# A three-block transformer kernel: in its first stage two held loads hang on other squares, one tile's weights load later, and all input sums run on Vector

## The chip, the cores and the metric

The kernel runs on one core of one Trainium2 chip. That core has a matrix engine (PE, with its weight loads as PEld), three engines for elementwise work (VectorE or DVE, ScalarE or ACT, GpSimd or POOL), and SP, which here issues all loads. Each engine works through its instructions in order. The metric is the device time of one execution in microseconds, as the median of several runs.

## The reference, cut to what matters

Two blocks run one after the other on 512 tokens of width 1024, in f32. Only the beginning of the first is touched by the change:

```python
mod = silu(c) @ ada_w + ada_b                # nine vectors of 1024
sh1, sc1, gt1, sh2, sc2, gt2, sh3, sc3, gt3 = split(mod, 9)
u = modulate(rmsnorm(h, norm1_w), sh1, sc1)  # h * (1 + scale) + shift
h = h + 0.5 * gt1 * swiglu(u, ffn1_w_in, ffn1_w_out)   # hidden width 2816
```

Behind it come the attention and retention mixers, a second feed-forward, and the second block with two more feed-forwards.

## The kernel before

**Numbers.** PE multiplies f32 values that are split into a high and a low half. A product is three matmuls: high by high, high by low, low by high. The halves of the input are `uh` and `ul`, those of a weight chunk `whi` and `wlo`. ACT makes each high half (`hi`, L230), DVE or POOL subtracts to get the low half (`lo`, L238 or L240).

**Start (method `start`).** All its instructions keep their written order on each engine (`pin`). SP loads the input as eight tiles `h[k]`. ACT squares each one, DVE adds the squares up, and `rstd` and `bcast` make the factor `R` from the sum. The vectors `sc1` and `sh1` come from eight "pairs" `apair` of 1 MB each (function `load`); DVE multiplies both halves of pair k by the row `cr`, which lies in PSUM, and sums (function `dots`, here: product k). With them DVE scales tile k (`unorm0`, tile `un`), ACT makes `uh` and a shifted copy, and POOL makes `ul`. Three pair buffers and three buffers for raw weights rotate, so a later load waits on SP until its buffer is free, and all that stands behind it on SP waits too. The loads of pairs 0 and 1 are held: `act` lets ACT write one element of the buffer first, so the load cannot be issued before ACT has come to that place. Four weight chunks, for hidden tiles 0 and 1 ("the first pair" of tiles; each tile has a chunk for the gate and one for the value), are loaded between the pairs (`wraw`) and split (`wsplit`). Behind product 5 ACT copies `cr` to SBUF as `crow`; product 6 waits for this copy.

**Feed-forward (method `ffn`).** Tiles 0 and 1 are multiplied in the order `FIRST`. Then `W=5` makes tiles 2, 3 and 4 run "whole": two chunks, 48 matmuls of 512 columns each. From tile 5 on the tiles run as units of seven half-size products, mixed with units of the output product. The units need sums and differences of four quarters of the input: `b` = `uh` + `ul` per quarter (L657), four differences (`bparts`, L497), and their halves; the fourth set rewrites a quarter of `uh` and `ul`, behind tile 4. In `CFG[0]` the letters of `UT` choose the engine of the four sums, `UE` of the four differences and `ULO` of the four low halves: `p` is POOL, `d` is DVE. Each unit also sums and subtracts its weights on POOL (`in_open`, tiles `ws`, `rb`, `raw`).

**Ada rows.** The other vectors of `mod` are computed row by row beside this: SP loads a row `araw` of 0.5 MB into one of two buffers and DVE multiplies it by `crow` and sums (L302). The list `ADA` says how many rows are issued at each place: its first entry ahead of tiles 0 and 1, then behind them, behind each of tiles 2 to 4, and then one per unit.

**Order.** Outside the pinned parts a scheduler with a model of the time decides the order on each engine. `issue_after(x)` keeps what is written in its block behind x on x's own engine only. `self.mark` holds two such instructions: the load of `identb`, last on SP in `start`, and the last `un` on DVE:

```python
x = self.unorm0(KT - 1, R)
self.mark = [nc.sync.dma_start(self.identb, a["constb"][:, 0:P]), x]
```

Of the kernel before, what the change touches and what calls it, by code (L numbers as in the profile page):

```python
# [17 lines left out]
S = 512  # L18
# [3 lines left out]

FIRST = [(k, j) for k in (0, 1) for j in (0, 1)] + [(k, j) for j in (2, 3) for k in (0, 1)] + [(k, j) for k in range(2, 8) for j in range(4)]
SPLIT = ((0, 4), (4, 4), (8, 4), (12, 4), (16, 6))
HP, ARB, ADA = 200, 2, (0, 3, 3, 2) + (1,) * 17

CFG = (dict(SENG='pppp', UT='pdpp', UE='ddpp', ULO='dddp', CF=(1, 1, 2, 4), W=5, LEAD=2),
       dict(SENG='pppp', UT='ddpd', UE='dddd', ULO='dddd', CF=(2, 2, 2, 4), W=3, LEAD=2),
       dict(SENG='pdpp', UT='pdpd', UE='ddpp', ULO='pdpp', CF=(1, 1, 2, 4), W=3, LEAD=2),
       dict(SENG='pppp', UT='pdpp', UE='ddpd', ULO='dddd', CF=(1, 1, 2, 4), W=3, LEAD=2))  # L30
# [127 lines left out]
class Builder:  # L158
# [232 lines left out]
    def norm(self, blk, st, a, sh=None, eng="dve"):  # L391
        c0, n = blk
        R = self.bcast(self.rstd(self.msq([st], n)[0], n), n)
        for k in range(KT):
            e = eng[k] if len(eng) == KT else "d"
            self.unorm(k, c0, n, a, sh, R, self.t(self.npool, [P, 264], F32, "unorm", bufs=3)[:, :n], {"p": "pool", "d": "dve"}[e])

    def unorm(self, k, c0, n, a, sh, R, u, eng="dve"):
        nc = self.nc
        uh, ul = self.uh[:, k, c0:c0 + n], self.ul[:, k, c0:c0 + n]  # L400
        nc.vector.scalar_tensor_tensor(u, self.h[:, k, c0:c0 + n], a[:, k:k + 1], R, op0=ALU.mult, op1=ALU.mult)
        if sh is None:
            self.hi(uh, u)
            self.lo(ul, u, uh, eng)
        else:
            nc.scalar.activation(uh, u, AF.Identity, bias=sh[:, k:k + 1])
            nc.vector.scalar_tensor_tensor(ul, u, sh[:, k:k + 1], uh.bitcast(F32), op0=ALU.add, op1=ALU.subtract)
# [72 lines left out]
    def out_open(self, wo, m, f0, nk):  # L480

        R = self.t(self.wp, [P, 1024], F32, "raw", bufs=3)
        for i in range(2):
            with self.tc.high_priority(HPD):
                self.nc.sync.dma_start(R[:, 512 * i:512 * i + nk * P], wo[m + i][:, f0 * P:(f0 + nk) * P])
        wh, wl = (self.t(self.wp, [P, 1024], F32R, x) for x in ("whi", "wlo"))
# [49 lines left out]
    def ffn(self, idx, wa, wb, wo, coef, first, blocks, last, stat, done, ada=(), late=False, half=None, opened=None, start=None, wl="dve"):  # L536
# [9 lines left out]
        (c0, n), (c1, _) = half  # L546
        self.cfg = CFG[idx]
        self.cf, whole_to, lead = (self.cfg[x] for x in ("CF", "W", "LEAD"))
        with ExitStack() as ctx:
# [10 lines left out]
            def close(f):  # L560

                g[f] = gtile()
                src = gx[f][:, :, :n]
                h, l = (x.rearrange("p (b n) -> p b n", b=2) for x in g[f])
                self.hi(h, src)
                self.lo(l, src, h)
# [53 lines left out]
            def whole(fs, ws, order=None):  # L620
                for bc, bn in first:
                    pts = self.group(ws, self.uh, self.ul, bc, bn, order=order)
                    for j, f in enumerate(fs):
                        if f not in gx:
                            gxt(f)
                        for b, c in ((0, c0), (1, c1)):
                            if bc <= c < bc + bn:
                                s = gx[f][:, b, :n]
                                nc.scalar.activation(s, pts[2 * j][:, c - bc:c - bc + n], AF.Silu)
                                nc.vector.tensor_tensor(s, pts[2 * j + 1][:, c - bc:c - bc + n], s, op=ALU.mult)  # L630

            if ada:
                ap = self.pool("ada", ctx=ctx)
            cst = ctx.enter_context(ExitStack())
            ws = start(cst) if start else [self.wchunk(w(f), 1024, wl) for f in range(2) for w in (wa, wb)]
            f1 = len(ws) // 2
            if ada:
# [33 lines left out]
                close(f)  # L671
            for f in range(f1, whole_to):
                with ExitStack() as c:
                    if start:
                        c.enter_context(self.tc.issue_after(self.mark[1].ins))
                    ws = [self.wchunk(w(f), 1024) for w in (wa, wb)]
                whole([f], ws)
                close(f)
                self.ada_after(ada.pop(0) if ada else 0)
# [392 lines left out]
    def ret(self, xp, mp, st, oh, ol, raw, other):  # L1072
# [15 lines left out]
        for i in range(N + AH + 3):  # L1088
# [31 lines left out]
            if 0 <= k < N:  # L1120
                t, r, j = units[k]
                n = S - P * j
                start = j == 0
                if start:
                    po = self.ps("po")
                for y in s_.pop(k):
                    mm(po[:, P * j:], st["rv"][:, j, 2 * t + r, :], y[:, :n], start=start, stop=True, skip_group_check=True)
                    start = False
                if j == 3:
                    if r == 0:  # L1130
                        ot = self.t(mp, [P, S], F32, "ot", bufs=1)
                    self.fold(mp, ot, r, po)
                    if r == 1:
                        late.append((i + 2, self.ret_norm(mp, t, st, ot, oh, ol)))
# [646 lines left out]
    def start(self, wsrc):  # L1781

        nc, a = self.nc, self.a
        nc.pin(True)
        c = self.t(self.ap, [1, D], F32, "c0")
        nc.sync.dma_start(self.vecs, a["vecs"])
        nc.sync.dma_start(c, a["crow"])
        nc.sync.dma_start(self.cst, a["consts"])
        for k in range(KT):
            nc.sync.dma_start(self.h[:, k, NM:L], a["xT"][k])  # L1790
        nc.scalar.activation(c, c, AF.Silu)
        self.sqrtset()

        cr = self.psum.tile([P, D], F32, tag="pl", name=self.nm("pl"), bufs=1)
        for i in range(2):
            nc.tensor.matmul(cr[:, S * i:S * i + S], self.con("ones")[0:1, :], c[:, S * i:S * i + S], start=True, stop=True)
        pt = self.ps("aux")
        raws = {}

        def load(k, gate=None):  # L1800

            raws[k] = self.t(self.ap, [P, 2, D], F32, "apair", bufs=3)
            if gate is not None:
                gate(raws[k][0:1, 0, 0:1])
            return nc.sync.dma_start(raws[k].rearrange("p a b -> p (a b)"), a["ada_c"][k])

        def act(o):
            nc.scalar.activation(o, self.eps[0:1, :], AF.Copy)

        def dots(k):  # L1810

            sc, sh = (self.mod[v][:, k:k + 1] for v in (1, 0))
            for j, m in ((0, sc), (1, sh)):
                nc.vector.scalar_tensor_tensor(raws[k][:, j], raws[k][:, j], 1.0, cr, op0=ALU.mult, op1=ALU.mult, accum_out=m)
            nc.scalar.activation(sc, sc, AF.Identity, scale=self.mod_w(1, k, 1), bias=s1[:, k:k + 1])
            nc.scalar.activation(sh, sh, AF.Identity, bias=self.vec("ada_b", k, 1))

        for k in range(KT):
            if k == 6:
                load(0, act)  # L1820
            sq = self.t(self.ap, [P, S], F32, "sqa0") if k == 0 else self.t(self.ap, [P, S], F32, "sq0", bufs=3)
            nc.scalar.activation(sq, self.h[:, k, NM:L], AF.Square)
            if k:
                nc.vector.tensor_tensor(acc, acc, sq, op=ALU.add)
            else:
                acc = sq
        for i in range(4):
            nc.tensor.matmul(pt[:, i:i + 1], acc[:, i * P:i * P + P], self.con("ones")[:, 0:1], start=True, stop=True)

        s1 = self.t(self.ap, [P, KT], F32, "s1")  # L1830
        nc.vector.scalar_tensor_tensor(s1, self.vec("ada_b", 8, 8), 1.0, self.vec("norm1_w"), op0=ALU.add, op1=ALU.mult)
        R = self.bcast(self.rstd(pt[:, 0:4], S), S)
        ws = [self.wraw(wsrc[0])]
        load(1, act)
        ws += [self.wraw(wsrc[1]), self.wraw(wsrc[2])]
        load(2)
        dots(0)
        ws[0] = self.wsplit(ws[0], self.wx)
        self.unorm0(0, R, lambda: ws.__setitem__(0, ws[0]("pool")))
        ws.append(self.wraw(wsrc[3]))  # L1840
        for k in range(1, KT):
            dots(k)
            if k < 6:
                load(k + 2)
            if k < 4:
                ws[k] = self.wsplit(ws[k], self.wx if k == 1 else None)
            if k > 1:
                self.unorm0(k - 1, R)
            if k < 4:
                ws[k] = ws[k]("pool")  # L1850
            if k == 5:
                nc.scalar.activation(self.crow, cr, AF.Copy)
        x = self.unorm0(KT - 1, R)
        self.mark = [nc.sync.dma_start(self.identb, a["constb"][:, 0:P]), x]
        return ws
# [79 lines left out]
```

## Time and profile before

| | us |
|---|---|
| median of 3 runs | 2374.49 |
| lowest and highest | 2372.78, 2375.73 |
| the profiled execution | 2369.6 |
| its span | 2367.8 |

The profile shows one execution. Its chain of work that ended last runs through PE for 72% of the span and through DVE for 12%. PE is busy for 2247.1 us, DVE for 1620.2 us, ACT for 1131.6 us and POOL for 927.9 us. The stage in question is the first 110 us. In the views an instruction is named by its line, the tile that it writes and the tiles that it reads; `x2` counts instructions that are merged in a row. The brackets give the engine's idle time before the instruction and what ended it. PEclk is the clock granted to PE, as a share of 2.4 GHz.

### The profile page before, as it was taken

How to read it: one execution, taken by the hardware profiler on the slowest of the kernel's cores; microseconds unless marked ns; L12 is line 12 of the kernel's file. 1: busy time of each engine (PE TensorE's matmuls, PEld its weight loads, DVE VectorE, ACT ScalarE, POOL GpSimd, SP SyncE). 2: the span in 40 equal slices, each digit the busy share in tenths (PEclk: the TensorE clock that was granted, in tenths of full speed). 3: DMA queues.
4: the chain of work that ended last, by engine and by line, in shares of the span. 5: the costliest groups of instructions: out<-in, count | busy, mean ns of one | idle time of the engine just before them, and what ended most of it. 6: DMA issues, size and time to landing. Idle time of an engine off the chain costs nothing.

```text
span 2367.8 us, 39220 instructions
## 1 busy us (share of the span) xinstructions
PE 2247.1 (95%) x15328; PEld 2073.3 (88%) x15328; DVE 1620.2 (68%) x2432; ACT 1131.6 (48%) x2005; POOL 927.9 (39%) x787
## 2 busy tenths in 40 slices
PE   6899999999999989999996999999999999999998
PEld 4799999888877879899996899999998888999998
DVE  6877776356665857766657776666578886866664
ACT  5344445355545234444445444444466664544443
POOL 4434442133332212544438643333334434544442
PEclk9999999999999999999997899999999999999999
DMA  8533336211143862333322133332322223232332
GB/s 298 169 125 120 124 103 188 75 37 36 56 141 95 261 214 72 107 107 99 107 71 81 35 100 107 99 99 70 124 84 63 71 68 107 92 97 98 101 94 83
DMA packets 95227, 253.29 MB, mean 107 GB/s; under 512 B 16641, under 2 KB 23425, under 8 KB 93762
## 3 DMA queue, kind: packets, MB, share of 16 engines
q1 hardware_dynamic: 95042, 250.79, 33.7%
q8 instruction: 120, 1.97, 0.3%
q14 instruction: 65, 0.53, 0.1%
HBM read 238.03 MB, written 6.29 MB: 103 GB/s over the span
## 4 chain that ended last, share of the span: by engine, by line
PE 72%; DVE 12%; DMA 5%; issue 5%; ACT 3%; POOL 3%; SPq 0%; DVEq 0%; ACTq 0%; POOLq 0%
PE mA L138 22%; PE mB L138 18%; PE mm L138 7%; PE pl L138 5%; PE at L138 3%; DVE wlo L238 3%; PE mA L270 2%; PE mA L271 2%; PE mA L272 2%; PE mB L272 2%; PE mB L271 2%; PE mB L270 2%; DMA araw<-in_ada_r_dram 2%; PE po L138 1%; PE tp L138 1%
## 5 line engine op out<-in xcount | busy, mean ns | idle before, releaser
L230 ACT ACTIVATE whi<-raw 128x1024 fp32r<-128x1024 f32 (+2 forms) x285 | 292.6, 1031 | 317.9 <-PE mB L138 119.7
L238 DVE TENSOR_TENSOR wlo<-raw,whi 128x1024 fp32r<-128x1024 f32 (+2 forms) x257 | 336.4, 1312 | 96.0 <-ACT whi L230 94.7
L138 PE MATMUL mA<-uh,whi 128*128 128x256 f32 (+2 forms) x1004 | 292.2, 291 | 18.9 <-ACT unorm L572 10.0
L138 PE MATMUL mA<-uh,wlo 128*128 128x256 f32 (+2 forms) x1004 | 290.1, 289 | 5.0 <-DVE wlo L238 3.4
L138 PE MATMUL mA<-ul,whi 128*128 128x256 f32 (+2 forms) x1004 | 289.7, 289 | 2.9 <-POOL ul L138 2.9
L463 POOL TENSOR_TENSOR ws<-raw,rb 128x512 f32<-128x512 f32 x74 | 107.3, 1450 | 289.4 <-DMA rb<-in_ffn_w_in_dram 97.4
L138 PEld LDWEIGHTS mA<-uh,whi 128*128 128x128 f32 x1004 | 191.3, 191 | 27.8 <-ACT unorm L572 14.5
L138 PEld LDWEIGHTS mA<-uh,wlo 128*128 128x128 f32 x1004 | 191.1, 190 | 8.1 <-DVE wlo L238 4.4
L138 PEld LDWEIGHTS mA<-ul,whi 128*128 128x128 f32 x1004 | 191.2, 190 | 6.7 <-POOL ul L138 4.4
L475 POOL TENSOR_TENSOR raw<-raw,ws 128x512 f32<-128x512 f32 x74 | 101.4, 1370 | 215.8 <-DVE wlo L238 126.4
L593 POOL TENSOR_TENSOR gx<-gx,unorm 128x256 f32<-128x256 f32 (+1 forms) x74 | 68.0, 918 | 224.8 <-ACT gx L592 224.8
L138 PE MATMUL mB<-uh,wlo 128*128 128x256 f32 (+2 forms) x524 | 153.1, 292 | 2.2 <-POOL wlo L138 2.2
L138 PE MATMUL mB<-uh,whi 128*128 128x256 f32 (+2 forms) x524 | 152.7, 291 | 0.0
L138 PE MATMUL mB<-ul,whi 128*128 128x256 f32 (+2 forms) x524 | 152.7, 291 | 0.0
L238 DVE TENSOR_TENSOR wlo<-rb,whi 128x1024 fp32r<-128x1024 f32 x74 | 113.5, 1534 | 45.5 <-ACT whi L230 45.5
L238 DVE TENSOR_TENSOR wlo<-ws,whi 128x1024 fp32r<-128x1024 f32 x74 | 126.2, 1706 | 17.1 <-ACT whi L230 16.9
L230 ACT ACTIVATE whi<-rb 128x1024 fp32r<-128x1024 f32 x74 | 77.9, 1052 | 105.2 <-PE mB L138 58.4
L138 PE MATMUL mm<-uh,whi 128*128 128x264 f32 (+2 forms) x368 | 125.0, 340 | 1.2 <-DVE sks L1504 1.2
L465 POOL TENSOR_TENSOR rb<-rb 128x512 f32<-128x512 f32 x74 | 125.0, 1689 | 1.1
L352 POOL TENSOR_TENSOR sqacc<-sqacc,sqt 128x256 f32<-128x256 f32 (+2 forms) x84 | 79.3, 965 | 113.6 <-ACT sqt L347 113.3
L238 DVE TENSOR_TENSOR gl<-gx,gh 128x512 fp32r<-128x512 f32 (+1 forms) x88 | 68.9, 786 | 75.9 <-ACT gh L230 75.9
L138 PE MATMUL mm<-uh,wlo 128*128 128x264 f32 (+2 forms) x368 | 120.8, 328 | 0.0
(537 smaller groups left out, 7717.8 us busy)
## 6 DMA issues: line engine op xcount, KB each, us to landing
araw<-in_ada_r_dram SPq DMA_DIRECT2D x56, 512.0 KB, 4.5
raw<-in_ffn_w_in_dram SPq DMA_DIRECT2D x52, 512.0 KB, 3.8
raw<-in_ffn_w_gate_dram SPq DMA_DIRECT2D x44, 512.0 KB, 3.8
rb<-in_ffn_w_up_dram SPq DMA_DIRECT2D x38, 512.0 KB, 3.6
rb<-in_ffn_w_in_dram SPq DMA_DIRECT2D x36, 512.0 KB, 3.6
raw<-in_wA_dram SPq DMA_DIRECT2D x36, 512.0 KB, 3.7
raw<-in_ffn_w_out_dram SPq DMA_DIRECT2D x64, 256.0 KB, 3.4
raw<-in_ffn_w_down_dram SPq DMA_DIRECT2D x64, 256.0 KB, 3.0
```

The lines of the kernel that those rows point to most:

```text
L138: ins = f(*args, **kw)
L230: nc.scalar.activation(out, src, AF.Copy)
L238: self.nc.vector.tensor_tensor(out, src, hi.bitcast(F32), op=ALU.subtract)
L270: mm(ps, wh, xh, start=first, stop=False)
L271: mm(ps, wh, xl, start=False, stop=False)
L272: mm(ps, wl, xh, start=False, stop=last)
L352: nc.gpsimd.tensor_tensor(st["acc"], st["acc"], s, op=ALU.add)
L463: E[3].tensor_tensor(s3, A[:, 0:512], b1, op=ALU.subtract)
L465: E[1].tensor_tensor(b1, b1, b2, op=ALU.add)
L475: E[4].tensor_tensor(a2, a2, s2, op=ALU.subtract)
L593: nc.gpsimd.tensor_tensor(y, y, u["z"], op=ALU.mult)
```

## The change

Five edits, all in the first feed-forward. In `CFG[0]` all letters of `UT`, `UE` and `ULO` become `d`: three sums, two differences and one low half go from POOL to DVE. `ADA` gets a second zero in front, so that no rows are issued behind the first pair and three, three, two behind tiles 2, 3 and 4. The chunks of tile 2 to 4 are kept behind both marks instead of the second alone, so on SP behind `identb`. In `start` pair 0 is held by the third square instead of the sixth, and pair 1 by the eighth square instead of the square root in `rstd`, whose lines move behind it.

```diff
-HP, ARB, ADA = 200, 2, (0, 3, 3, 2) + (1,) * 17
-
-CFG = (dict(SENG='pppp', UT='pdpp', UE='ddpp', ULO='dddp', CF=(1, 1, 2, 4), W=5, LEAD=2),
+HP, ARB, ADA = 200, 2, (0, 0, 3, 3, 2) + (1,) * 17
+
+CFG = (dict(SENG='pppp', UT='dddd', UE='dddd', ULO='dddd', CF=(1, 1, 2, 4), W=5, LEAD=2),
...
             for f in range(f1, whole_to):
                 with ExitStack() as c:
-                    if start:
-                        c.enter_context(self.tc.issue_after(self.mark[1].ins))
+                    for m in self.mark if start else ():
+                        c.enter_context(self.tc.issue_after(m.ins))
                     ws = [self.wchunk(w(f), 1024) for w in (wa, wb)]
...
         for k in range(KT):
-            if k == 6:
+            if k == 3:
                 load(0, act)
...
-        R = self.bcast(self.rstd(pt[:, 0:4], S), S)
         ws = [self.wraw(wsrc[0])]
         load(1, act)
+        R = self.bcast(self.rstd(pt[:, 0:4], S), S)
         ws += [self.wraw(wsrc[1]), self.wraw(wsrc[2])]
```

What this does to the order shows on two engines. On SP, behind the loads of pairs 3 and 4 (`apair`), with `raw` the chunks of tiles 2, 3 and 4 in turn and `araw` the ada rows:

```order
 L138 DMA apair_210<-in_ada_c_dram 128x2048
-L245 DMA raw_460<-in_ffn_w_in_dram 128x1024
 L138 DMA apair_226<-in_ada_c_dram 128x2048
 L138 DMA apair_242<-in_ada_c_dram 128x2048
-L245 DMA raw_466<-in_ffn_w_in_dram 128x1024
 L138 DMA apair_254<-in_ada_c_dram 128x2048
 L138 DMA identb_84<-in_constb_dram 128x128
```

The two chunks of tile 2 leave their places between the pairs; in the new order they are the first rows behind `identb`, ahead of the first two ada rows.

On DVE, behind the last `un`, before the change:

```order
L302 SCALAR_TENSOR_TENSOR araw_402,mod_15_90<-araw_402,crow_74 128x1024
L302 SCALAR_TENSOR_TENSOR araw_405,mod_15_90<-araw_405,crow_74 128x1024
L238 TENSOR_TENSOR wlo_463<-raw_460,whi_462 128x1024
L238 TENSOR_TENSOR wlo_469<-raw_466,whi_468 128x1024
L657 TENSOR_TENSOR b_95_435<-uh_82,ul_83 128x1024
L302 SCALAR_TENSOR_TENSOR araw_408,mod_15_90<-araw_408,crow_74 128x1024
L302 SCALAR_TENSOR_TENSOR araw_531,mod_15_90<-araw_531,crow_74 128x1024
L497 TENSOR_TENSOR b_94_433<-b_95_435,b_94_433 128x1024
L138 TENSOR_TENSOR gx_391<-mB_292,gx_391 128x256 x2
L238 TENSOR_TENSOR wlo_543<-raw_540,whi_542 128x1024
```

and with it, where `wlo_454` and `wlo_460` belong to tile 2 and `wlo_534` to tile 3:

```order
L238 TENSOR_TENSOR wlo_454<-raw_451,whi_453 128x1024
L238 TENSOR_TENSOR wlo_460<-raw_457,whi_459 128x1024
L302 SCALAR_TENSOR_TENSOR araw_522,mod_15_90<-araw_522,crow_74 128x1024
L302 SCALAR_TENSOR_TENSOR araw_525,mod_15_90<-araw_525,crow_74 128x1024
L657 TENSOR_TENSOR b_91_424<-uh_82,ul_83 128x1024
L657 TENSOR_TENSOR b_92_426<-uh_82,ul_83 128x1024
L657 TENSOR_TENSOR b_93_428<-uh_82,ul_83 128x1024
L657 TENSOR_TENSOR b_94_430<-uh_82,ul_83 128x1024
L138 TENSOR_TENSOR gx_391<-mB_292,gx_391 128x256 x2
L302 SCALAR_TENSOR_TENSOR araw_528,mod_15_90<-araw_528,crow_74 128x1024
L497 TENSOR_TENSOR b_91_424<-b_92_426,b_91_424 128x1024
L238 TENSOR_TENSOR wlo_534<-raw_531,whi_533 128x1024
```

DVE now does all four sums in a row, one ada row fewer ahead of tile 3's first low half, and eight instead of nine ada rows ahead of tile 4's.

## Rows read from the trace of the kernel before

**Rows 1.** Profile page, part 1: busy us of each engine (share) and instructions.
```profile
PE 2247.1 (95%) x15328; PEld 2073.3 (88%) x15328; DVE 1620.2 (68%) x2432; ACT 1131.6 (48%) x2005; POOL 927.9 (39%) x787
```
**Rows 2.** Timeline of PE, tiles 2 to 4: start, us, instruction [idle before, releaser].
```profile
57.35 0.40 PE L270 MATMUL mA<-uh,whi 128*128 128x512 f32 x1
...
68.72 0.40 PE L271 MATMUL mA<-ul,whi 128*128 128x512 f32 x1
...
70.12 0.50 PE L272 MATMUL mA<-uh,wlo 128*128 128x512 f32 x1 [1.00 <-DVE wlo L238]
...
71.92 0.72 PE L272 MATMUL mB<-uh,wlo 128*128 128x512 f32 x1 [0.84 <-DVE wlo L238]
...
88.19 0.50 PE L272 MATMUL mA<-uh,wlo 128*128 128x512 f32 x1 [4.02 <-DVE wlo L238]
...
89.99 0.80 PE L272 MATMUL mB<-uh,wlo 128*128 128x512 f32 x1 [0.84 <-DVE wlo L238]
...
90.58 0.63 PE L270 MATMUL mA<-uh,whi 128*128 128x512 f32 x1
...
95.70 0.50 PE L270 MATMUL mA<-uh,whi 128*128 128x512 f32 x1
```
**Rows 3.** Chain of waits, where the units begin: start, us, what.
```profile
102.91 1.41 PE mA L138 x12
```
**Rows 4.** Windows: PE, PEld, DVE, ACT, POOL busy, PEclk, DMA share, GB/s.
```profile
72.00:74.00 2.00, 2.00 (x5) 1.62 (x6) 2.00 (x3) 0.34 (x1) 0.00 (x0) 0.51 0.73 240
...
92.00:94.00 2.00, 2.00 (x7) 1.54 (x6) 1.42 (x3) 0.07 (x1) 2.00 (x2) 0.50 1.01 381
```
**Rows 5.** Timeline of DVE, same columns as rows 2.
```profile
55.14 3.44 DVE L657 TENSOR_TENSOR b<-uh,ul 128x1024 f32<-128x1024 f32 x1
...
58.51 3.42 DVE L302 SCALAR_TENSOR_TENSOR araw<-araw,crow 128x1024 f32<-128x1024 f32 x1
...
65.22 1.22 DVE L497 TENSOR_TENSOR b<-b,b 128x1024 f32<-128x1024 f32 x1
...
67.02 3.05 DVE L238 TENSOR_TENSOR wlo<-raw,whi 128x1024 fp32r<-128x1024 f32 x1
...
78.69 3.43 DVE L302 SCALAR_TENSOR_TENSOR araw<-araw,crow 128x1024 f32<-128x1024 f32 x1
...
85.77 1.22 DVE L302 SCALAR_TENSOR_TENSOR araw<-araw,crow 128x1024 f32<-128x1024 f32 x1 [1.08 <-DMA araw<-in_ada_r_dram]
...
88.72 1.21 DVE L238 TENSOR_TENSOR wlo<-raw,whi 128x1024 fp32r<-128x1024 f32 x1
...
103.17 1.23 DVE L238 TENSOR_TENSOR wlo<-rb,whi 128x1024 fp32r<-128x1024 f32 x1 [4.38 <-ACT whi L230]
```
**Rows 6.** Timeline of POOL.
```profile
54.10 10.10 POOL L657 TENSOR_TENSOR b<-uh,ul 128x1024 f32<-128x1024 f32 x3
...
77.71 3.32 POOL L497 TENSOR_TENSOR b<-b,b 128x1024 f32<-128x1024 f32 x1 [8.72 <-DVE b L497]
...
90.16 1.51 POOL L463 TENSOR_TENSOR ws<-raw,rb 128x512 f32<-128x512 f32 x1 [9.13 <-DMA rb<-in_ffn_w_in_dram]
```
**Rows 7.** Timeline, POOL, SP, DVE and PE to 42 us; one window; SP later.
```profile
21.33 2.36 POOL L138 TENSOR_TENSOR wlo<-raw,whi 128x1024 fp32r<-128x1024 f32 x1
...
23.71 0.33 SPq L138 DMA_DIRECT2D raw<-in_ffn_w_in_dram  x1
...
30.24 1.22 DVE L138 SCALAR_TENSOR_TENSOR apair<-apair,pl 128x1024 f32<-128x1024 f32 x1 [1.64 <-DMA apair<-in_ada_c_dram]
...
30.00:40.00 10.00, 7.73 (x19) 5.27 (x20) 9.01 (x15) 7.00 (x14) 8.42 (x5) 1.00 1.02 420
...
38.86 0.50 PE L138 MATMUL mB<-uh,wlo 128*128 128x512 f32 x1 [1.11 <-POOL wlo L138]
...
41.85 1.22 DVE L138 SCALAR_TENSOR_TENSOR apair<-apair,pl 128x1024 f32<-128x1024 f32 x1 [2.38 <-ACT crow L138]
...
83.71 0.86 SPq L456 DMA_DIRECT2D rb<-in_ffn_w_in_dram  x2
```

## Prediction

> **What bounds the kernel now.** I read the busy table first: PE is busy for 95% of the span, DVE for 68%, POOL for 39% [rows 1]. With PE that full, a change beside it gains only where PE waits, so the next view is PE in order of time over the stage that the diff touches. Two things are to be seen. Tile 2 starts at 57.35 us and the units behind tile 4 at 102.91 us [rows 2, 3]: 45.6 us. In them PE stops four times, always for a low half `wlo` from DVE: before 70.12, 71.92, 88.19 and 89.99 us, 1.00 + 0.84 + 4.02 + 0.84 = 6.7 us [rows 2]. After the second and after the fourth stop the granted clock is about one half, the 1.2 GHz level [rows 4]; PE had nearly stood through the two stops before. A matmul starts every 0.232 us at full clock (50 starts from 57.35 to 68.72) and every 0.427 us then (13 starts from 90.58 to 95.70) [rows 2]; some 8 slow ones after the first pair of stops and 13 after the second cost 21 x 0.2 = 4.2 us. So 10.9 us of this stage are DVE's lateness. Without it 3 x 48 matmuls x 0.232 = 33.4 us are left.
>
> Why is DVE late? Its rows say so [rows 5]: a 128x1024 instruction takes 1.21 or 1.22 us in some places and 3.05 to 3.44 us in others. The long ones all lie beside POOL's 128x1024 sums [rows 6]: three input sums from 54.10 us, 10.10 us long together, and differences, of which the one at 77.71 took 3.32 us. The lengths fit taking turns: 2.3 us for POOL and 1.14 us for DVE, end to end, make 3.44.
>
> **The change, part by part**, on the profiled execution: span 2367.8 us and 1.8 us around it, 2369.6 us, which is 4.9 us under the median of the runs, 2374.5 us. I carry the difference over to the median.
>
> *Input sums on Vector.* Up to the low half of tile 4's second weight (88.72 us) DVE takes over three sums and two differences: 5 x 1.14 us (start to start; 1.22 as a row) = +5.7 us. No row shows a sum of line 657 on DVE alone. Its bounds are 1.22 us (the difference of line 497 at 65.22, same size) and 3.44 us (the sum at 55.14, beside POOL) [rows 5]; I take the first, since POOL is then empty and the second has POOL as its reason. The sixth added instruction, the low half of the rewritten quarter, comes behind 88.72 in DVE's order; DVE now stands 4.38 us there before 103.17 [rows 5], which hides it, and it costs 1.14 us if that gap closes. What goes: five stretched rows, 3.44 + 3.42 (58.51) + 3.42 (its twin directly behind) + 3.05 + 3.43, less 5 x 1.22: -10.7 us. Two `wlo` ahead of them stay beside POOL's last two `ul` and stay long.
>
> *Ada rows.* The list moves one of nine rows from before tile 4's split to the units: -1.15 us, and with it DVE's wait of 1.08 us for that row's load before 85.77 [rows 5]. In the units DVE gets one row more beside PE's work; with DVE at 68% I cost it at nothing, and at 1.2 us without cover.
> The Trainium skill speaks on these rows (Vector Engine (DVE) Microarchitecture Reference, section 7, Points that are easy to get wrong): a scalar_tensor_tensor with two SBUF sources that aren't bf16 runs at half rate. An ada row is one and takes 1.22 us at 85.77, as long as the plain difference at 65.22, so the trace does not agree; by the rule the row moved away would bring 2.3 us instead of 1.15.
>
> *Held loads.* The loads of pairs 0 and 1 go some microseconds earlier. Product 0 still waits for the reciprocal, which hangs on all eight squares. Products 1 and 2 come 2 to 3 us earlier, an estimate from 1.05 MB per pair at 420 GB/s. Product 3 does not: its load stands on SP behind the fourth raw weight, issued at 23.71 us when POOL's `wlo` of 21.33 us has freed its buffer [rows 7], and nothing moves that. From 23.71 to 30.24 us [rows 7] is the latency of an idle queue plus 1.5 MB, so product 3 stays there. Behind it every step goes at DVE's own pace, with the stop of 2.38 us for the copy `crow` before 41.85 us as before. A gain is bounded by DVE's wait of 1.64 us before 30.24; I take 0.
>
> *Third tile's weights behind the last pair.* Two loads of 0.5 MB leave the full stretch (420 GB/s from 30 to 40 us [rows 7]); product 5, which now waits a little for its pair, no longer does: -0.25 us. The cost: they land behind pair 7. Data of the fourth weight starts at about 26.5 us (30.24 less 1.57 MB at 420 GB/s); 0.5 + 5 x 1.05 + 0.5 MB behind that end at 41.5 us. ACT reaches the first one's `whi` behind the scale of product 6, at 41.85 + 1.2 - 0.25 = 42.8 us. Queued behind it on ACT stand the shift and `uh` of the sixth square, and for those wait POOL's `ul` and PE. The margin is 1.3 us; a rate 8% lower takes it.
> The Trainium skill (DMA: Bandwidth & Descriptors, section Where 436 GB/s comes from) lets the HBM side bind at about 358 GB/s. The row at 420 does not agree; by the rule ACT would wait 1.3 us there, and that much of the gain could go.
>
> *Sum on DVE*, at the end of tile 4's second `wlo`: +5.7 - 10.7 - 1.15 - 1.08 - 0.25 = -7.5 us: 89.9 becomes 82.4, and tile 4's first ends at 80.6. Tile 3's two, counted along DVE's new order, end at about 64 and 67, ahead of PE.
>
> *Sum on PE.* PE's work on `k` = 1 and on the third weight comes up to 3 us earlier with product 2, the fourth weight's low half does not; so before 38.86 us PE waits some 4 us where it waits 1.11 now [rows 7]. In the trace a longer standstill led to the low clock both times. Tile 2 starts between 57.0 (clock kept) and 59.8 (14 slow matmuls). Tile 3's stops and their slow stretch go. If PE is on time it reaches tile 4's first `wlo` at 79.6, waits 1.0 and 1.1 us and runs 8 slow matmuls behind: 82.4 + 43 x 0.232 + 1.6 = 94.0 for the end. If it comes 1.6 us later, the waits shrink to 0.6 us and the clock holds: 92.6. I take 93.4 against 102.9: -9.5 us. Behind that PE is full in the units and their order is the same, so the gain stays: 2374.5 - 9.5 = 2365.0.
>
> **Rivals.**
> 1. *The units are not ready at 93 us.* SP holds `rb` behind an ada row; it goes at 83.71 now, and POOL starts on it at 90.16 [rows 6, 7] with four instructions of about 1.5 us, to 96. If it does not move along, the products on the differences wait until 97 and those on the sum longer: gain near 5 us, 2369.5. Against: the ada row in front waits for DVE's seventh ada product, which along the new order ends near 76.
> 2. *DVE's long rows are not POOL's doing* but belong to their places (the operands, DMA writes beside them). Then none of the 10.7 us goes, the five sums add 5.7, the ada terms give back 2.2 and the loads 0.25: DVE and with it PE are 3.2 us later, 2377.7; with sums at 3.44 us it is 14.7. It decides from the first sum on DVE that takes over 3 us with POOL idle. Against: 1.22 us at 65.22, 1.0 us after POOL's last sum ended.
> 3. *The held loads do carry*: product 3 comes 1.6 us earlier and all behind it, and PE restarts without a slow stretch: gain 12, 2362.5. For: DMA is full from 30 us on. Against: 23.71.
> 4. *The gain is given back later*: a stop of 5 to 9 us on PE behind the units leaves no change, 2372. PE's order differs in a handful of rows where the norms follow; for a stop of that size nothing in the trace speaks.
>
> **How the numbers follow.** Forecast 0.66 (2363.5 to 2367), rival 1 0.14, rival 2 0.05, rival 3 0.05, rival 4 0.10. The limit of 0.2%, 4.7 us, is about what a measurement of this kernel can tell from no change; below it lies 2369.8. Faster: 0.66 + 0.05 + two thirds of rival 1 = 0.80; same: the rest of rival 1 and rival 4, 0.15; slower 0.05. The range leaves out rival 2 and half of rival 4: from 2361.8 (PE with no stop at all, 57 + 33.4 = 90.4, 12.5 us and a little) to 2370.5.
>
> **What would show it.** In the profile after: line 657 on DVE four times at 1.2 us (rival 2 if 3); POOL empty between 54 and 80 us; PE's stops for `wlo` in tiles 2 to 4 under 2.5 us together; the first unit at 92 to 94.5 us; product 3 at 30.2 us (rival 3 if under 29); `rb` issued near 77 (rival 1 if over 82). I am wrong if the first unit starts there and the span does not follow.

## The result, and the profile after

| | before | changed |
|---|---|---|
| median, first comparison (4 runs each) | 2373.64 us (2372.35 to 2375.73) | 2358.68 us (2354.16 to 2359.27) |
| ratio, 95% interval | | 0.9937 (0.9924 to 0.9950) |
| profiled execution, span | 2367.8 us | 2352.4 us |

The change made the kernel 15.0 us faster in this comparison. The forecast was 2365.0 us, 9.5 us faster; the median lies 6.3 us under the forecast and 3.1 us under the low end of its range. Two later comparisons of the same pair, among the experiments below, gave 9.8 and 9.0 us.

The trace of the changed kernel shows the stage (the time from tile 2's first matmul to the first unit) as forecast in kind. First Vector (start, us, instruction, what ended the idle time before it), against [rows 5, 7]:

```profile
29.69 1.22 DVE L138 SCALAR_TENSOR_TENSOR apair<-apair,pl 128x1024 f32<-128x1024 f32 x1 [3.55 <-DMA apair<-in_ada_c_dram]
...
54.29 4.62 DVE L657 TENSOR_TENSOR b<-uh,ul 128x1024 f32<-128x1024 f32 x4
...
78.46 1.22 DVE L238 TENSOR_TENSOR wlo<-raw,whi 128x1024 fp32r<-128x1024 f32 x1
...
80.26 1.22 DVE L238 TENSOR_TENSOR wlo<-raw,whi 128x1024 fp32r<-128x1024 f32 x1
```

The four sums take 4.62 us together, 1.14 from start to start, where one alone took 3.44 beside GpSimd [rows 5]. Tile 4's second low half ends at 81.5 us; before it ended at 89.9.

GpSimd and SP, against [rows 6, 7]:

```profile
51.00 2.27 POOL L138 TENSOR_TENSOR ul<-un,uh 128x512 fp32r<-128x512 f32 x1
80.30 2.31 POOL L463 TENSOR_TENSOR ws<-raw,rb 128x512 f32<-128x512 f32 x1 [27.03 <-DMA rb<-in_ffn_w_in_dram]
```
```profile
75.57 0.86 SPq L456 DMA_DIRECT2D rb<-in_ffn_w_in_dram  x2
```

GpSimd is empty from 53.3 to 80.3 us, and the units' weights `rb` are asked for 8 us earlier than before, so they moved along with the rest.

TensorE: its waits from 57 to 92 us (what it waited for: us in total, times, longest), the one row with a stop, and the chain where the units begin, against [rows 2, 3]:

```profile
PE mB L272 <- DVE wlo L238: 0.4, 1, 0.4
```
```profile
81.53 0.50 PE L272 MATMUL mB<-uh,wlo 128*128 128x512 f32 x1 [0.38 <-DVE wlo L238]
```
```profile
91.77 1.41 PE mA L138 x12
```

Four stops of 6.7 us have become one of 0.4 us. Tile 2 starts at 57.55 us and the units at 91.77: 34.2 us in place of 45.6. Windows over the same tiles (PE, PEld, DVE, ACT, POOL busy, PEclk, DMA share, GB/s) have no low clock left, against [rows 4]:

```profile
72.00:74.00 2.00, 2.00 (x10) 1.64 (x9) 2.00 (x3) 1.12 (x2) 0.00 (x0) 1.00 0.77 215
80.00:92.00 12.00, 11.62 (x52) 9.14 (x52) 11.26 (x11) 6.47 (x10) 8.41 (x4) 1.00 0.50 175
```

So the first unit starts 11.1 us earlier, not 9.5. The span shrank by 15.4. Two questions were open: where the other 4.3 us arose, and which parts of the change made the 11.1.

### The profile page after: what moved, and what is told of

The parts are those of the page before. It is cut to its first block, busy times and chain, and to the rows that moved or that the text cites. A ratio compares the mean times of both kernels' runs of the same rounds, so it can differ in the third digit from the quotient of the medians.

```text
span 2352.4 us, 39213 instructions
## 1 busy us (share of the span) xinstructions
PE 2237.8 (95%) x15328; PEld 2066.3 (88%) x15328; DVE 1618.9 (69%) x2438; ACT 1131.6 (48%) x2005; POOL 908.9 (39%) x781
## 4 chain that ended last, share of the span: by engine, by line
PE 71%; DVE 13%; DMA 5%; issue 5%; ACT 3%; POOL 3%; SPq 0%; DVEq 0%; ACTq 0%; POOLq 0%
PE mA L138 22%; PE mB L138 18%; PE mm L138 6%; PE pl L138 5%; PE at L138 3%; DVE wlo L238 2%; DMA araw<-in_ada_r_dram 2%; PE mA L271 2%; PE mA L270 2%; PE mA L272 2%; PE mB L272 2%; PE mB L271 2%; PE mB L270 2%; PE tp L138 1%; PE po L138 1%
## 5 line engine op out<-in xcount | busy, mean ns | idle before, releaser
L238 DVE TENSOR_TENSOR wlo<-ws,whi 128x1024 fp32r<-128x1024 f32 x74 | 125.5, 1695 | 15.7 <-ACT whi L230 15.4
```

What stands on the lines that cost most here:

```text
L238: self.nc.vector.tensor_tensor(out, src, hi.bitcast(F32), op=ALU.subtract)
```

## The experiments

In all kernels two instants can be read: tile 2's start and the first unit. The table holds them, the stage between them, what the span has behind the first unit ("behind"), and the medians. "Before" is the kernel before in the same comparison. The first unit is read from the chain of waits, as in [rows 3]; its first matmul starts 0.17 us earlier (91.60 for 91.77), and one expectation below counts from there.

| kernel | tile 2 | units | stage | behind | median (before) |
|---|---|---|---|---|---|
| before, profile 1 | 57.35 | 102.91 | 45.6 | 2264.9 | 2373.64 |
| before, profile 2 | 56.40 | 101.84 | 45.4 | 2271.3 | 2374.92, one run |
| changed, profile 1 | 57.55 | 91.77 | 34.2 | 2260.6 | 2358.68 (2373.64) |
| changed, profile 2 | 57.05 | 91.31 | 34.3 | 2262.8 | 2360.98 (2370.82) |
| changed, profile 3 | 58.90 | 92.47 | 33.6 | 2267.6 | 2361.11 (2370.10) |
| letters alone | 57.56 | 93.46 | 35.9 | 2264.8 | 2359.94 (2370.82) |
| all but the letters | 58.26 | 101.73 | 43.5 | 2264.4 | 2368.95 (2370.82) |
| GpSimd busy beside | 57.48 | 98.36 | 40.9 | 2267.3 | 2366.61 (2372.06) |
| old ada list | 57.42 | 93.89 | 36.5 | 2260.1 | 2360.39 (2372.06) |
| old held loads | 57.84 | 94.22 | 36.4 | 2267.2 | 2361.08 (2372.06) |
| old mark | 58.05 | 92.60 | 34.6 | 2265.5 | 2359.93 (2370.10) |
| pair 3 first | 54.80 | 90.06 | 35.3 | 2268.6 | 2359.39 (2372.06) |
| pair 3 first, early crow | 53.44 | 87.92 | 34.5 | 2264.9 | 2351.36 (2370.10) |

**The same kernels again.** No edit. The question is whether the 4.3 us behind the units belong to the change.

> The changed kernel once more, word for word. Its trace starts the units at 91.77 us and needs 2260.6 us from there to the end of the span; the kernel before needs 2264.9 us from its 102.91. Theory A: the 4.3 us behind the first unit are the phase in which one execution meets the stalls of the mixer and the low clock; then a second execution starts the units at 91.8 +- 0.3 again but needs between 2260 and 2266 us behind them. Theory B: the few rows that the planner put in another order (26 of 15100 on TensorE near 395 and 1245 us, some on Vector and Scalar) shorten what follows; then 2260.6 +- 1.0 comes again.

> The kernel before once more. Theory A (phase of one execution): units from 102.9 +- 0.3 us, the stretch behind them anywhere between 2260 and 2266 us, the low clock (now at 480, 540 and 580 us) at other places. Theory B (order of rows): 2264.9 +- 1.0 us and the low clock at the same places.

The units started at 91.31 and 101.84 us, 0.5 and 1.1 us earlier than in the first profiles, so the start of the units scatters by more than the 0.3 us that theory A allowed. Behind them came 2262.8 and 2271.3 us. The second is 5 us beyond even theory A's span, and 6.4 us from the first profile of the very same kernel. Theory B asked for 2260.6 and 2264.9 +- 1.0 and fails on both. In medians the pair now differed by 9.8 us: ratio 0.9956 (0.9938 to 0.9973).

**Letters alone, and all but the letters.** The kernel before with one line changed, and the changed kernel with that line put back:

```diff
-CFG = (dict(SENG='pppp', UT='pdpp', UE='ddpp', ULO='dddp', CF=(1, 1, 2, 4), W=5, LEAD=2),
+CFG = (dict(SENG='pppp', UT='dddd', UE='dddd', ULO='dddd', CF=(1, 1, 2, 4), W=5, LEAD=2),
```

> The kernel before with the new letters alone: the four sums, the differences and the low half on Vector; ada rows, held loads and the marks as before. By the sum on record the letters are worth 10.7 - 5.7 = 5.0 us of Vector, the ada row 1.15 + 1.08 and the earlier product 0.25; on TensorE the units should start at 94 to 97 us, against 91.77 with the whole change and 102.91 before, and the four sums take 1.1 to 1.2 us each. Rival: the letters alone are nearly all (units at 92 to 93), the other edits nothing. The other rival: the letters do not work alone, since POOL's sums only give way to the nine ada rows (units later than 98).

> The changed kernel with the old letters: sums and differences on GpSimd and Vector as before, but the ada list, the held loads and both marks as changed. By the sum on record these edits are worth 2.5 us of Vector, and some stops of TensorE with them: units at 98.5 to 101.5 us. Rival (the letters are nearly all): units at 102 to 103 us. Theory A: from there 2260 to 2266 us to the end. Theory B: this kernel has the changed kernel's rows near 395 us and the old ones near 1245 us; if the first set carries the 4.3 us it needs 2260.6, if the second does, 2264.9.

The letters alone: units at 93.46, between the 94 to 97 of the sum and the 92 to 93 of the rival; the four sums 4.62 us together; ratio 0.9956 (0.9939 to 0.9973), as good as the whole change in the same comparison. All the rest without them: units at 101.73, just beyond the expected 98.5 to 101.5, ratio 0.9992 (0.9983 to 1.0002), no difference that stands out from the scatter. Vector and GpSimd of the latter still show the pattern of before:

```profile
55.01 3.43 DVE L657 TENSOR_TENSOR b<-uh,ul 128x1024 f32<-128x1024 f32 x1
```
```profile
53.96 10.11 POOL L657 TENSOR_TENSOR b<-uh,ul 128x1024 f32<-128x1024 f32 x3
```

So the letters are worth 9.7 us of stage (45.6 to 35.9) and the rest 1.7 us on top of them (35.9 to 34.2).

**GpSimd busy beside.** The changed kernel with the three old sums given to GpSimd a second time, to a spare tile. The order of all other engines' rows stays the changed kernel's, to the last row:

```diff
+            if start:
+                for k, c in ((0, c0), (4, c0), (4, c1)):
+                    t = self.t(tp, [P, 4, n], F32, "bz")
+                    nc.gpsimd.tensor_tensor(t, self.uh[:, k:k + 4, c:c + n].bitcast(F32), self.ul[:, k:k + 4, c:c + n].bitcast(F32), op=ALU.add)
             for o, i, j in UO:
```

> The changed kernel with three idle sums given to GpSimd where the old ones stood: same operands and size, written to a spare tile that nobody reads; every other engine's rows stand as in the changed kernel. It does three operations more than the kernel needs. Theory (Vector's long rows are GpSimd's doing): the three take 10 us together as the old ones did, three of Vector's 128x1024 rows beside them take 3.4 us in place of 1.2, and Vector is 6.6 us later at the fourth tile's second low half (88.0 for 81.4). TensorE stops there for about 6 us and runs some matmuls at the low clock behind it: from the start of the third tile to the units 41 to 44 us in place of 34.2, the whole +7 to +10 us against the changed kernel. Rival 2 of the prediction (the length belongs to the rows or their operands): Vector's rows stay at 1.2 us, 34.2 +- 0.5 us, and no change.

Vector's four sums, tile 4's second low half, and GpSimd's idle sums:

```profile
54.26 11.25 DVE L657 TENSOR_TENSOR b<-uh,ul 128x1024 f32<-128x1024 f32 x4
...
86.85 1.21 DVE L238 TENSOR_TENSOR wlo<-raw,whi 128x1024 fp32r<-128x1024 f32 x1
```
```profile
53.20 10.09 POOL L662 TENSOR_TENSOR bz<-uh,ul 128x1024 f32<-128x1024 f32 x3
```

The four sums take 11.25 us in place of 4.62: Vector lost 6.6 us to three instructions whose result nobody reads, and its low half ends at 88.1 as expected. The stage is 40.9 us, 6.7 more than the changed kernel's and just under the expected 41 to 44. TensorE's stops are 4.7 us in all where about 6 were expected, and they lie at tiles 3 and 4 instead of at one place. The median is 5.4 us under before (ratio 0.9973, 0.9961 to 0.9985); the mean of its five runs, 2366.0, is 6.6 us over the changed kernel's 2359.3 (13 runs), just under the expected 7 to 10 and as much as the stage. This shows the cause: the long rows are GpSimd's doing, and rival 2 falls.

The run speaks against theory B as well: with the changed kernel's order in every other engine it has 2267.3 us behind the units, not 2260.6. The third profile of the changed kernel itself has 2267.6.

> The changed kernel a third time. So far its profiles start the units at 91.60 and 91.15 us and need 2260.8 and 2262.9 us behind them; eight other profiles need 2260 to 2271, one of them with all other engines' rows equal to the changed kernel's. Theory: what stands behind the units is the same work for all kernels, 2267 to 2270 us in the median of several executions, and it differs by execution with the granted clock; then this kernel's median is 11.2 +- 2 us under the kernel before (the stage's 45.3 less 34.1). Rival: the 15.0 us of the first comparison were the change's own, 4 us of it behind the units; then 14 to 16 us again.

The pair differed by 9.0 us here (ratio 0.9959, 0.9946 to 0.9971), 0.2 us outside the theory's 11.2 +- 2 and far from the rival's 14 to 16. What an execution has behind the units goes with the clock that it is granted there. The same 180 us of the changed kernel in its three profiles, columns as above, PEclk third from the end:

```profile
440.00:620.00 180.00, 169.96 (x1169) 155.47 (x1169) 109.58 (x282) 96.98 (x249) 57.81 (x76) 0.99 0.13 41
```
```profile
440.00:620.00 180.00, 171.16 (x1153) 156.48 (x1152) 108.45 (x278) 95.31 (x245) 57.36 (x75) 0.96 0.13 40
```
```profile
440.00:620.00 180.00, 171.41 (x1132) 157.18 (x1131) 105.22 (x270) 93.21 (x238) 56.24 (x73) 0.94 0.14 43
```

Same program, same time: 1169, 1153 and 1132 matmuls, at a granted clock of 0.99, 0.96 and 0.94. TensorE stood 10.0, 8.8 and 8.6 us in these stretches, so the later two do not owe their lower counts to longer waits. Over the whole time behind the units, the low clock level holds for 78, 87 and 97 us in these three traces, and for between 73 us (old ada list) and 104 us (before, profile 2) in all 13; those two have the shortest and the longest "behind" of the table, and the correlation of the two quantities is 0.86.

The 37 runs of the kernel before in the four comparisons lie between 2366.1 and 2375.9 us with a mean of 2371.3; all 13 of the changed one between 2354.2 and 2362.9 with a mean of 2359.3. The difference of the means is 12.0 us, with a standard error of 0.8 if every run counts as independent of the others, and the stage's 11.4 (45.6 less 34.2) lies within that error. By comparison, the means differ by 16.1, 11.0 and 9.8 us, which is further apart than the runs inside each would make likely (standard errors of 1.4 to 1.6). In the first one the kernel before lay 2.5 us over its mean of all runs and the changed one 1.6 us under its own. Whether that was chance or belongs to that comparison is not shown.

The Trainium skill (TensorE: Matmul & The Clock Gate, Part 1: The HAM clock gate) says, of the matmuls at a kernel's start, that the number at the low rate differs between runs of one kernel, and it advises against fitting a certain count. The three rows show such a difference in the middle of a kernel.

**Old ada list.** The changed kernel with `ADA = (0, 3, 3, 2) + (1,) * 17`.

> The changed kernel with the old list of ada rows: nine in place of eight ahead of the fifth tile's split. By the sum on record one row costs Vector 1.15 us and the wait for its load up to 1.08: from the third tile's start to the units 35.3 to 36.5 us in place of 34.2. Rival: the Vector engine has the room, 34.2 to 34.8.

The stage is 36.5 us, 2.3 more, as expected. TensorE's stops and the window behind them:

```profile
81.25 0.50 PE L272 MATMUL mA<-uh,wlo 128*128 128x512 f32 x1 [0.94 <-DVE wlo L238]
...
83.65 0.50 PE L272 MATMUL mB<-uh,wlo 128*128 128x512 f32 x1 [1.44 <-DVE wlo L238]
```
```profile
84.00:86.00 2.00, 2.00 (x10) 1.64 (x9) 2.00 (x2) 1.08 (x2) 2.00 (x2) 1.00 0.91 312
```

These stops are close to those that the forecast had for the changed kernel, 1.0 and 1.1 us, and the clock stays at 1.00 behind them: the 8 slow matmuls of the forecast do not come. The row's own price is made up otherwise than I had it: Vector is 2.1 us later at tile 4's second low half, 1.15 us for the row and 0.22 us for the wait for its load, and 0.67 us for two small instructions that close a vector of eight rows (L315 and L295, 0.07 and 0.60 us from start to start).

**Old held loads.** The changed kernel with `if k == 6` and with `R` ahead of the first raw weight.

> The changed kernel with the held loads at the old places (seventh square, broadcast ahead of the second one). By the prediction this is worth nothing: product 3 still waits for its pair behind the fourth raw weight at 29.7 to 30.3 us, third tile at 57.0 to 58.3, units 34.2 +- 0.4 us later. Rival 3 (the early loads carry): third tile at 58.5 us or later.

Product 3 started at 31.06 us, later than the expected 29.7 to 30.3, and the stage took 36.4 us where 34.2 +- 0.4 was expected; the third tile's start, 57.84, does not bear out rival 3 either. Over all kernels product 3 has no clear side: with the old loads it started at 30.24, 29.29, 29.80 and 31.06 us, with the new ones at 29.25 to 30.42 (seven profiles). Its mean differs by 0.3 us, less than the scatter. So whether the lateness of this one execution belongs to the old loads is not shown. What the run does show is how 1.4 us of lateness on Vector became 2.2 us of stage. Vector's second low half and GpSimd's first row of the units:

```profile
81.61 2.33 DVE L238 TENSOR_TENSOR wlo<-raw,whi 128x1024 fp32r<-128x1024 f32 x1
```
```profile
81.57 1.28 POOL L463 TENSOR_TENSOR ws<-raw,rb 128x512 f32<-128x512 f32 x1 [26.95 <-DVE gx L630]
```

GpSimd began 0.04 us ahead of Vector, and Vector's row took 2.33 us. In the changed kernel the pair starts the other way round, Vector at 80.26 and GpSimd at 80.30, and it is GpSimd's row that takes 2.31 us while Vector's takes 1.22. Whoever comes first goes at its own pace and the other waits it out. The Trainium skill (SBUF — State Buffer, Summary: rules for kernel authors) states this: where Vector has two SBUF inputs and GpSimd reads SBUF, the second to issue is blocked until the first is done. These four rows agree.

**Old mark.** The changed kernel with the third tile's weights behind `self.mark[1]` alone.

> The changed kernel with the third tile's weights held back by the last product alone, as before, and not by the last pair's load too. By the sum on record this edit is worth 0.25 us of Vector (product 5 no longer waits for its pair): units 0.1 to 0.5 us later than 91.4 counted with the same third-tile start, products 5 to 7 with a wait for their pairs of up to 1 us. Rival (the transfers in between hold up more): products 5 to 7 wait over 2 us together and the units start at 93 us or later.

The stage is 34.6 us, 0.3 more than the changed kernel's; Vector's waits for pairs are 6.4 us in all against 6.2, and the median is no different. The 0.25 us fits, though so small a difference is within the scatter of the stage (33.6 to 34.3 us over the changed kernel's profiles).

**Pair 3 first, and an early crow.** By the prediction the held loads gain nothing, since pair 3 stands behind the fourth raw weight. These two runs change that order, and the second also makes the copy `crow` where Vector waits for a pair anyway:

```diff
+        load(3)
         ws.append(self.wraw(wsrc[3]))
         for k in range(1, KT):
             dots(k)
-            if k < 6:
+            if 1 < k < 6:
                 load(k + 2)
...
-            if k == 5:
+            if k == 1:
                 nc.scalar.activation(self.crow, cr, AF.Copy)
```

> The changed kernel with the load of pair 3 issued ahead of the fourth raw weight, which waits for its buffer until 23.39 us. If that buffer is what holds the pair, product 3 starts at 25.5 to 27.5 us in place of 29.69, the 3.0 us stop of TensorE before 38.29 us shrinks to under 1.5 us, the third tile starts at 54 to 56 us in place of 57.55, the units at 88.5 to 90.5, and the whole gains 1.5 to 3 us on the changed kernel. Rival: the memory is full there and the pair's 1 MB only comes later in the queue of transfers (product 3 at 28.5 to 30): third tile at 57 to 58 us, no change. Second rival: TensorE is earlier but Vector is not, and the stop goes to the fourth tile's low halves: third tile at 54 to 56, units at 91 to 92.

> The changed kernel with the load of pair 3 ahead of the fourth raw weight, and the copy crow made behind pair 1, where Vector waits for a pair anyway, in place of behind pair 5. Vector's stop of 2.4 us for that copy should go. Theory: third tile at 54.3 to 55.3 us, no stop of TensorE at the fourth and fifth tile, from the third tile to the units 33.5 to 34.2 us, units at 88.0 to 89.2, and the whole 2 to 3.5 us under the changed kernel in the same comparison. Rival: with Vector out of the way the next limit is the fifth tile's weights or the units' own first weights on GpSimd: units at 89.5 to 91.5, no change to the whole.

In the first, SP issues pair 3 directly behind pair 2, by 17.6 us in place of 23.8, and Vector's product 3 starts 3.2 us earlier:

```profile
12.76 4.83 SPq L138 DMA_DIRECT2D apair<-in_ada_c_dram  x2
```
```profile
26.50 1.21 DVE L138 SCALAR_TENSOR_TENSOR apair<-apair,pl 128x1024 f32<-128x1024 f32 x1
```

This shows that the place behind the fourth raw weight was what held product 3. Tile 2 starts at 54.80 us and the units at 90.06, both as the theory had it. Vector still stands 2.4 us for `crow`, and part of the gain turns into stops at tile 4 (1.1 us), as the second rival had it in kind. The expected 1.5 to 3 us of the whole do not show: the median, 2359.39, does not stand out from the changed kernel's. With the early copy, ACT's row falls into a gap and Vector's waits up to 58 us lose it:

```profile
21.97 1.00 ACT L138 ACTIVATE crow<-pl 128x1024 f32<-128x1024 f32 x1
```
```profile
DVE apair L138 <- DMA apair<-in_ada_c_dram: 4.5, 3, 2.7
```
```profile
87.92 1.41 PE mA L138 x12
```

The units start at 87.92 us, 3.9 before the changed kernel's first profile and just ahead of the expected 88.0 to 89.2. The stage itself is 34.5 us, with one stop of 0.64 us, where 33.5 to 34.2 and no stop were expected: all of the gain lies ahead of tile 2, which starts at 53.44. The median is 2351.36 us (2349.54 to 2356.86), ratio to before 0.9928 (0.9916 to 0.9941) where the changed kernel has 0.9959 (0.9946 to 0.9971) in the same comparison: it beats both. It also beats its expectation of 2 to 3.5 us under the changed kernel: the medians lie 9.8 us apart, the means 7.3. The earlier units explain 3.4 to 4.6 of that, by which profile of the changed kernel one takes. The rest would lie behind the units; its one profile has 2264.9 us there, in the midst of the changed kernel's three, so where the rest arose is not shown.

## Why the prediction missed

The forecast had the right cause and the right place. Three of its terms had the wrong size: the base, the sum on PE and, by less, the sum on DVE. For the scatter of single executions it had no term.

- *The base.* "I carry the difference over to the median": the base of 2374.5 us came from three runs. The mean of 37 runs is 2371.3. Of the 6.3 us of the miss 3.1 are this step, 1.6 are the sum on PE below, and the remaining 1.6 lie behind the units and in the four executions of the first comparison, 0.7 us under the mean of 13. Counted within the first comparison alone, whose kernel before has a median of 2373.64, the base makes only 0.9 us of the miss and what lies behind the units 3.8. Either way, this step and the scatter of executions put the time outside the range, and not the stage: its 11.1 us alone would have made 2363.4 us, inside it. Three runs of a kernel whose executions lie up to 9.8 us apart do not give a base to 2 us, and the range, which reached down only to a TensorE without stops, took no account of that.
- *Sum on DVE*, 82.4 us for tile 4's second low half: it ended at 81.5. From product 3 on Vector needed 7.9 us less than before (59.7 to 51.8), where the sum said 7.5; the 0.4 us are the same two small instructions (L315 and L295), which stood ahead of the ada row's wait before the change and have moved to the units. The other 0.55 is product 3 itself, at 29.69 for 30.24, within the scatter of its start. The term stands: Vector's added rows take the 1.14 us that the 5.7 assumed, and the rows behind the 10.7 us are no longer stretched. The two rows that GpSimd's last `ul` still stretch are now two ada rows (2.33 and 2.31 us) and not, as forecast, the two low halves, at the same price.
- *Sum on PE*, 93.4 us: the units started at 91.77. This is the step that failed in the mechanism. Vector was 0.9 us earlier than forecast and met TensorE almost on time, so the stops were 0.4 in place of 2.1 us; and the 8 slow matmuls behind them, 1.6 us, were wrong even for stops of that size, as the old ada list shows (2.4 us of stops, clock 1.00). I had read "a stop, then the low clock" from two cases in one trace and made it a term. Ahead of tile 2 the same reading came true: behind TensorE's stop of 3.00 us before 38.29 us, where the forecast had some 4, the granted clock is 0.50 from 40 to 42 us, and tile 2 still started at 57.55, near the early end of the forecast's 57.0 to 59.8. The reading of the trace before was short too: 10.9 us of lateness and 33.4 of work make 44.3 us and not 45.6. The changed kernel's third profile, which has no stop, needs 33.6 us, so stops and low clock had cost 12.0.
- *"The gain stays"*: it does. Stage and total agree to 1 us over 13 and 37 runs. The 4.3 us extra of the first pair of profiles go with the clock of single executions (the low level holds for 91 us behind the units before, 78 after). Profiles of one and the same kernel lie 6 to 7 us apart there, and over all runs only 0.6 us, less than the error, are left for a change behind the units. The forecast had no term for this, and it is why the spans of the first two profiles differ by 15.4 us.
- *Held loads 0, third tile's weights 0.25*: borne out as far as can be told. The third tile's first high half, on ACT, began at 42.53 us without a wait for its load, where the forecast had 42.8 and a margin of 1.3. All edits but the letters give 1.7 us of stage on top of them, and the old ada list alone takes 2.3 away again; by themselves they make no measurable total. The sixth added instruction, forecast as hidden, cost nothing: TensorE has no stop from 92 to 110 us.
- *Rivals.* 1 (units not ready) did not occur: `rb` was issued at 75.57. Its reading of the trace before was short: GpSimd's four instructions end at 97.4 us there, not at 96. 2 is refuted by the idle sums. 3 came nearest in time, 2362.5, by another way: product 3 started at 29.69, not under 29. 4 did not occur.

What stays open: why one execution is granted 0.99 and another 0.94 over the same stretch, why the three comparisons of the pair differ as they do, and whether the last kernel owes the part of its gain that its earlier units do not explain to the order of its rows. None of these was tried.

## What to carry to other kernels

Moving work from GpSimd to a busier Vector can free Vector, if the two run side by side on SBUF operands: count the stretched rows against the added ones before looking at busy shares. Give the engines a margin where one waits for the other: close to the balance 1.4 us of lateness became 2.2 by a collision here. And take the base and its scatter from as many runs as there are, and check a gain at the end of the stage that was changed before reading the span of one execution.

## What the runs showed of the hardware

- Of a GpSimd 128x512 row and a Vector 128x1024 row that start 0.04 us apart, the one that starts second takes about 1.1 us longer (81.57 and 81.61; 80.26 and 80.30).
- Stops of 0.94 and 1.44 us with the old ada list, or of 2.05 in the kernel with the letters alone, left TensorE's clock at 1.00; stops of 1.00 and 0.84 us [rows 2] were followed by the 1.2 GHz level, 0.51 [rows 4]. With GpSimd busy beside, both occurred in one trace: 0.39 and 1.98 us were followed by 0.50 from 74 us on, 1.47 and 0.84 by 1.00:

```profile
72.59 0.50 PE L272 MATMUL mB<-uh,wlo 128*128 128x512 f32 x1 [1.98 <-DVE wlo L238]
...
88.12 0.50 PE L272 MATMUL mB<-uh,wlo 128*128 128x512 f32 x1 [0.84 <-DVE wlo L238]
```
```profile
74.00:76.00 2.00, 2.00 (x6) 1.62 (x5) 2.00 (x3) 1.06 (x1) 0.00 (x0) 0.50 0.99 381
...
88.00:90.00 2.00, 1.88 (x8) 1.56 (x9) 2.00 (x3) 1.09 (x3) 1.92 (x2) 1.00 1.00 337
```

So the length of the stops does not tell the level behind them.
